# A hybrid attention block on one core: p and its weights prepared among the heads, z by pairs of token tiles, convolution ahead of token sums

## The chip, the core and the metric

The kernel runs on one core of a Trainium2 chip. The metric is the device time of one execution in microseconds (us). The core has a matrix engine (PE), three elementwise engines (DVE, ACT and POOL), an engine that issues transfers (SP), and 16 DMA engines. PE writes its products into banks of 128x512 floats in the accumulation memory (PSUM); a bank can be written again only when whoever reads it is done.

## What is computed

One layer of a streaming encoder on 512 tokens with 1024 features, all in fp32, with x held transposed (features by tokens):

```
h = rms_norm(x);  z = h @ w_in            # q latent | kv latent | rope key | diff q | diff k | diff v
x = x + concat[8 MLA heads, 4 differential heads](z) @ w_out
h2 = rms_norm(x)
x = x + (silu(causal_conv3(h2 @ w_gate)) * (h2 @ w_up)) @ w_down        # 2816 = 22 blocks of 128
x = x + sigmoid(rms_norm(x) @ w_ple_gate) * (p @ w_ple_proj)            # p: 512 x 256
```

The attention is causal by chunks of 64 tokens. For a tile of 128 queries only the keys up to it are computed.

## The kernel before

**Products.** Every large product is made of three (`mm3`, L151): each factor is split into a high part, which PE takes directly, and the rest (low), and PE sums high·high, high·low and low·high (L154 to L156). A split is a cast on ACT (`hi`, `h`) and a subtraction on DVE, or on POOL where `eng=G` stands (`lo`, `l`). `load_w` (L142) loads a raw weight block of 128x1024 and splits it; `hl` (L786) does so in the later stages.

**Order.** PE runs in the order in which the program is written (L98). DVE, ACT and POOL run so only in two regions: from the start to slot 4 of the MLA heads (opened at L218 and closed by `region.__exit__` under `i == 4`), and from the last output products to the end of the token preparation (L792). Outside of them a scheduler orders the three. Each engine works through its own queue in order, so an instruction that waits holds back all behind it.

**Banks and buffers.** PSUM is divided by tags: `acc` 2 banks, `lg` 3, `tp` 2, `ob` 1. SBUF tiles come from pools by tag with a number of buffers each. A load into a buffer waits until the last use of the tile that was there.

**Stages.**
1. Start: `WARM` = 17 small products on ones keep PE busy until the first weights are there. Then `zA` (the latents) over four pairs of feature blocks (`kq`) and four token tiles (`t`).
2. `zd` (the differential heads' q, k, v: three groups `c` of 512 columns) is cut into units of six matmuls by `zd_units` (L398). They fill gaps: `pump(n)` puts n units into PE's order. For c = 1 and 2 the units run token tile by token tile, each over its four weight blocks. `zd_norm(c)` scales group c: a chain of small DVE instructions and four of 128x512.
3. The MLA heads run in 32 slots (head h, query tile t). A slot issues the logits (`ml`) of the next slot, at t = 0 and 1 the transposes of q and k for the next head (`qT`, `kT`, evacuated by ACT and DVE into `st`), then some zd units, the transposes of the probabilities (`pTm`, evacuated as `pt` by ACT or DVE in turn) and the products with v (`mo`). The first three slots also load and split w_d for zd's group 1 (`zw1`), and slot 4 runs `zd_norm(0)`.
4. The differential heads run in 16 slots (`dl`, `pmd`, `pTd`, `do`, transposes `d0T` and `d1T`), with the output projection (`o`, weights `hi_o` and `lo_o`) as filling. The eight last sums of the projection follow, each with `add_x` on DVE and a square on ACT (`nsq`), summed on DVE in `nr`.
5. p and w_ple_proj are split in this last stretch, after the attention's buffers are released; POOL makes their three low parts. `pp_unit(b)` makes the eight products p @ w_ple_proj, which are put aside by ACT (`ppo`) and a store; all of them use the two `acc` banks. Between them lie the norm's products (`norm_r`, `norm_b`), and then DVE and ACT prepare h2 (`tokens`: `xg`, `b1`, `b2`).
6. Feed-forward blocks 0 to 2 (`plain`) take all eight products for g and u. Block 3 and later (`gu_units`) take seven half-sized ones (`11`, `12`, `S2`, `S4`, `S3`, `S1`, `22`), which need sums of tokens (`token_sums`: `bt`) and sums of weights (`w_prep`: `s`, `wT`). `gate_post` is the convolution: it reads the bank of g (ACT `cv`, then two DVE instructions). `up_post` multiplies by u and splits the result (`ah`, `al`). The down projection (`dn`) runs as filling, with weights of `down_w`.
7. The last norm and the gate.

The kv tile (`kvb`: keys and values of the MLA heads) lies in pool `att`; b1, b2 and bt lie in the feed-forward pools.

Of the kernel before, what the change touches and what calls it, by code (L numbers as in the profile page):

```python
# [11 lines left out]
F32 = mybir.dt.float32  # L12
# [43 lines left out]
WARM = 17  # L56
# [38 lines left out]
def hybrid_block(ctx: ExitStack, tc: tile.TileContext, a: dict, out: bass.AP):  # L95
# [6 lines left out]
    sm = ctx.enter_context(tc.tile_pool(name="sm", bufs=2))  # L102
    att = tc.alloc_tile_pool(name="att", bufs=1, side="left")
# [22 lines left out]
    def kv_tile(name, dtype=F32):  # L126
        return att.tile([P, NT, H, 160], dtype, tag="kv", name=name)
# [219 lines left out]
    for kq in range(4):  # L347
        for t in range(NT):
            mm3(zps[t][:, :416], xblocks(2 * kq, 2 * kq + 2, t, *wa[kq], 416), kq == 0, kq == 3)
# [48 lines left out]
    def zd_units():  # L398
        for c in range(3):
# [9 lines left out]
            else:  # L409
                ws = zw1 if c == 1 else [load_w(a["w_d"][c, kq], 1024, f"d{c}{kq}") for kq in range(4)]  # L410
                for t in range(NT):
                    ps = bank("acc", f"zd{c}{t}")
                    for kq in range(4):
                        mm3(ps, xblocks(2 * kq, 2 * kq + 2, t, *ws[kq], 512), kq == 0, kq == 3)
                        if kq == 3:
                            zd_out(c, t, ps)
                        yield
# [296 lines left out]
    for i, (h, t) in enumerate(slots):  # L714
        if i + 1 < len(slots):
            mla_logits(*slots[i + 1])
        if i < 3:
            zw1.append(load_w(a["w_d"][1, i + 1], 1024, f"d1{i + 1}"))
        if i == 4:
            region.__exit__(None, None, None)  # L720
            zd_norm(0)
        if h + 1 < H and t < 2:
            (mla_q, mla_k)[t](h + 1)
# [39 lines left out]
    for dq in (2, 3):  # L763
        wo2[dq] = wo_w(1, dq)
    order = (0, 4, 1, 5, 2, 6, 3, 7)
# [28 lines left out]
    ptw = hl(raw_w(a["pT"], "rA", "pT", bufs=2), "wA", "pT", bufs=2, eng=G)  # L794
    wpp = [hl(raw_w(a["w_pp"][i], "rS", f"pp{i}", bufs=3), ("wS", "wT")[i], f"pp{i}", eng=G) for i in range(2)]
# [15 lines left out]
    for b in order:  # L811
# [7 lines left out]
        square(b)  # L819
    square(None)  # L820
# [26 lines left out]
    def pp_unit(b):  # L847
        ps, w = bank("acc", f"pp{b}"), wpp[b // 4]
# [22 lines left out]
    def w_prep(f):  # L871
# [3 lines left out]
        s24 = ffn2.tile([P, 1024], F32, tag="s24", name=f"s24_{f}")  # L875
        V.tensor_tensor(s24[:, :512], ra[:, :512], rs_[:, 512:], op=ALU.add)
        V.tensor_tensor(s24[:, 512:], ra[:, 512:], s24[:, :512], op=ALU.add)
        w = {"22": hl(raw_w(gu(f, 2, 3), "r22", f, 512), "w22", f, 512)}
        for keys, t in ((("11", "12"), wa_), (("S2", "S4"), hl(s24, "wT", f)), (("S3", "S1"), hl(rs_, "wS", f))):
# [144 lines left out]
    for k in range(K2):  # L1024
        token_sums(k)
# [205 lines left out]
```

## Time and profile before

| | us |
|---|---|
| three timed runs | 678.59, 679.49, 679.68 (median 679.49) |
| the profiled execution | 677.74 |
| its span in the trace | 676.0 |
| mean granted PE clock | 0.986 |

The trace belongs to the profiled execution. Its span begins with the first recorded instruction and ends with the last; 1.74 us of the execution's time lie around it. Times in rows count from the start of the span. A row of a timeline gives the start, the length, the engine, the line, the instruction with what it writes and reads, its shape, and in brackets how long the engine stood idle ahead of it and which instruction released it. A 512-column matmul is recorded with 0.39 us but the next one starts 0.23 us later, since they are pipelined. The clock is the share of full speed that PE was granted.

In order of time, the stages lie at: zA from 7 us, the MLA heads from about 60, the differential heads from about 160, the last sums of the output from 248, the products of p from 256, the feed-forward from 274 and the last gate from about 640.

### The profile page before, as it was taken

The page shows a single profiled execution, that of the slowest core. Times are in us where ns is not written, and L with a number is a line of the kernel's source. Part 1 is how long each engine was busy: PE and PEld are TensorE (multiplying, and loading weights), DVE is VectorE, ACT ScalarE, POOL GpSimd, SP SyncE. Part 2 cuts the span into 40 slices and gives each one's busy share as a digit, 9 for nine tenths or more (in the row PEclk, how much of TensorE's full clock was granted, in tenths as well). Part 3 has the DMA queues.
Part 4 walks back from the last instruction along what each step waited for, and adds up shares of the span by engine and source line. Part 5 has one row for each costly group of instructions (what it writes and reads, how often), then busy time and mean ns, then how long its engine had stood idle before and what let it go on. Part 6 is the DMA issues. An engine that isn't in the chain of part 4 may idle for free.

```text
span 676.0 us, 10426 instructions
## 1 busy us (share of the span) xinstructions
PE 651.0 (96%) x3942; PEld 574.8 (85%) x3942; DVE 495.0 (73%) x938; ACT 359.5 (53%) x623; POOL 64.7 (10%) x94
## 2 busy tenths in 40 slices
PE   9999699999999998989999999999999999999997
PEld 9987488888878786868899999999999999988886
DVE  6989636747779857997867768676868687768543
ACT  7496435636666545755545546464645455546311
POOL 2900040001010031011000010000000000000000
PEclk9999889999999998989999999999999999999999
DMA  8240124305200047656746465655557463431121
GB/s 306 78 157 31 64 80 150 99 1 201 80 1 1 1 157 202 208 134 178 166 119 194 110 172 140 168 150 152 168 119 196 114 196 112 142 125 36 51 85 48
DMA packets 29914, 82.64 MB, mean 122 GB/s; under 512 B 3101, under 2 KB 4125, under 8 KB 29737
## 3 DMA queue, kind: packets, MB, share of 16 engines
q1 hardware_dynamic: 23816, 69.17, 31.3%
q0 software_dynamic: 5616, 12.33, 10.4%
q8 instruction: 31, 0.51, 0.3%
q10 hardware_dynamic: 432, 0.49, 0.2%
q14 instruction: 19, 0.15, 0.1%
HBM read 77.77 MB, written 5.52 MB: 123 GB/s over the span
## 4 chain that ended last, share of the span: by engine, by line
PE 77%; DVE 13%; ACT 6%; issue 2%; DMA 1%; ACTq 0%; DVEq 0%
PE dn L156 6%; PE dn L155 6%; PE dn L154 6%; PE gx L156 4%; PE gx L155 4%; PE gx L154 4%; PE g L154 3%; PE g L155 3%; PE g L156 3%; PE mo L568 2%; PE zd L155 2%; PE pg L154 2%; PE pg L155 2%; PE pg L156 2%; PE zd L156 2%
## 5 line engine op out<-in xcount | busy, mean ns | idle before, releaser
L156 PE MATMUL dn<-ah,lo_dn 128*128 128x512 f32 x144 | 56.2, 390 | 0.0
L155 PE MATMUL dn<-al,hi_dn 128*128 128x512 f32 x144 | 56.1, 390 | 0.0
L154 PE MATMUL dn<-ah,hi_dn 128*128 128x512 f32 x144 | 56.0, 389 | 0.0
L869 POOL DMA_DIRECT2D rS<-in_w_gu x19 | 22.9, 1205 | 266.4 <-DVE lo_dn L148 100.2
L154 PE MATMUL zd<-hi_d,xh 128*128 128x512 f32 x96 | 40.8, 425 | 2.8 <-ACT hi_d L147 2.8
L189 DVE TENSOR_TENSOR wTl<-s,wTh 128x1024 fp32r<-128x1024 f32 x19 | 23.3, 1225 | 27.3 <-ACT wTh L188 27.3
L155 PE MATMUL zd<-lo_d,xh 128*128 128x512 f32 x96 | 39.1, 408 | 1.3 <-DVE lo_d L148 1.3
L616 DVE TENSOR_TENSOR x<-x,dn 128x512 f32<-128x512 f32 x44 | 30.0, 681 | 10.7 <-PE dn L156 10.6
L188 ACT CAST wAh<-rA 128x1024 fp32r<-128x1024 f32 x22 | 23.0, 1046 | 22.1 <-PE g L155 21.4
L997 DVE SCALAR_TENSOR_TENSOR cv<-u,cv 128x512 f32<-128x512 f32 x22 | 15.2, 690 | 25.0 <-PE u L156 25.0
L555 DVE TENSOR_REDUCE nm<-ml 128x1 f32<-128x128 f32 (+3 forms) x32 | 15.5, 486 | 23.8 <-PE ml L156 23.6
L156 PEld LDWEIGHTS dn<-ah,lo_dn 128*128 128x128 f32 x144 | 27.0, 188 | 5.6
L154 PEld LDWEIGHTS dn<-ah,hi_dn 128*128 128x128 f32 x144 | 27.1, 188 | 5.0
L189 DVE TENSOR_TENSOR wAl<-rA,wAh 128x1024 fp32r<-128x1024 f32 x22 | 26.9, 1225 | 6.0 <-ACT wAh L188 6.0
L155 PEld LDWEIGHTS dn<-al,hi_dn 128*128 128x128 f32 x144 | 27.0, 188 | 5.0
L989 ACT ACTIVATE cv<-g,cols 128x512 f32<-128x512 f32 x22 | 17.1, 776 | 24.5 <-DVE g L977 24.5
L189 DVE TENSOR_TENSOR wSl<-rS,wSh 128x1024 fp32r<-128x1024 f32 x21 | 25.7, 1225 | 4.4 <-ACT wSh L188 4.4
L558 ACT ACTIVATE pm<-ml,nm,rq 128x128 f32<-128x128 f32 (+3 forms) x32 | 19.7, 617 | 15.8 <-DVE nm L556 15.7
L188 ACT CAST wTh<-s 128x1024 fp32r<-128x1024 f32 x19 | 19.9, 1048 | 15.0 <-PE g L155 15.0
L661 ACT ACTIVATE pmd<-pmd,nmd 128x128 f32<-128x128 f32 (+3 forms) x32 | 17.9, 559 | 18.8 <-DVE nmd L660 16.7
L154 PE MATMUL g<-b2h,wAh 128*128 128x256 f32 (+1 forms) x88 | 26.3, 299 | 0.7 <-ACT g L960 0.7
L154 PE MATMUL o<-yh,hi_o 128*128 128x512 f32 x64 | 26.7, 418 | 0.0
(469 smaller groups left out, 2268.1 us busy)
## 6 DMA issues: line engine op xcount, KB each, us to landing
rA<-in_w_gu SPq DMA_DIRECT2D x22, 512.0 KB, 3.6
rS<-in_w_gu SPq DMA_DIRECT2D x22, 512.0 KB, 3.6
rS<-in_w_gu POOLq DMA_DIRECT2D x19, 512.0 KB, 6.5
raw_dn<-in_w_down SPq DMA_DIRECT2D x18, 512.0 KB, 6.4
raw_d<-in_w_d SPq DMA_DIRECT2D x12, 512.0 KB, 3.5
r<-in_w_gu SPq DMA_DIRECT2D x19, 256.0 KB, 3.9
raw_o<-in_w_out SPq DMA_DIRECT2D x8, 512.0 KB, 4.2
rS_pg<-in_w_pg SPq DMA_DIRECT2D x6, 512.0 KB, 4.3
```

What stands on the lines that cost most here:

```text
L154: TE.matmul(ps, xh, wh, start=first and i == 0, stop=False, skip_group_check=again)
L155: TE.matmul(ps, xh, wl, start=False, stop=False, skip_group_check=again)
L156: TE.matmul(ps, xl, wh, start=False, stop=last and i == n - 1, skip_group_check=again)
L188: S.copy(h_, src)
L189: return (eng or V).tensor_tensor(l_, src, _f32(h_), op=ALU.subtract)
L555: V.reduce_max(nm, ps[:, :n], axis=AX.X, negate=True)
L558: S.activation(pm[:, :n], ps[:, :n], AF.Exp, bias=nm, scale=r, accum_out=mla["ssum", h // 2][:, t, h % 2:h % 2 + 1])
L616: V.tensor_tensor(xb(b), xb(b), ps, op=ALU.add)
L661: S.activation(pm[:, :n], pm[:, :n], AF.Exp, bias=nm, scale=-1.0, accum_out=s0 if m == 0 else s1)
L869: nc.gpsimd.dma_start(sums[f].rearrange("p (i c) -> p i c", i=2), a["w_gu"][f][:, :2048].rearrange("p (i c) -> p i c", i=2)[:, :, :512], a ...
L989: S.activation(cv, g, AF.Identity, bias=cols[:, C_CB + f:C_CB + f + 1], scale=cw[2])
L997: V.scalar_tensor_tensor(cv, u, sign, cv, op0=ALU.mult, op1=ALU.mult)
```

## The change

It has eight parts; all keep what is computed.

- Five warm-up products fewer, and the first pair of feature blocks of zA runs feature block by feature block over all four token tiles.
- A pool `kvp` of its own holds the kv tile. After the heads the same buffer takes the split p and the first half of w_ple_proj (`pk`), then the high part of the token sums, then that of the last norm's result.
- zd's groups 1 and 2 run by pairs of token tiles: weight block by weight block, over two tiles in two banks.
- `zd_norm(0)` moves from slot 4 to slot 8, behind the next head's k; in the first slots the transposes of q and k stand ahead of the weight loads in the program.
- `pk` is loaded and split (ACT and DVE) before the last output products are written, so that the scheduler puts it among the differential heads. The second half of w_ple_proj is split on DVE and ACT behind the seventh output sum. The eight products use seven banks, and two more of them stand ahead of the norm's second half or between other steps.
- In `w_prep` the sums of weights are made in place, in the raw tile.
- In blocks 0 to 2 the token sums stand behind the convolution, two by two. The loads of down weights wait until a block's `al` is done.
- In block 4 the product `S4` stands ahead of the `22` product of block 3.

```diff
-WARM = 17
+WARM = 12
...
+    kvp = tc.alloc_tile_pool(name="kvp", bufs=1, side="left", reuse_waits="tile")
...
     for kq in range(4):
+        if kq == 0:
+            for j in range(2):
+                for t in range(NT):
+                    mm3(zps[t][:, :416], xblocks(0, 2, t, *wa[0], 416)[j:j + 1], j == 0, False)
         for t in range(NT):
-            mm3(zps[t][:, :416], xblocks(2 * kq, 2 * kq + 2, t, *wa[kq], 416), kq == 0, kq == 3)
+            if kq:
+                mm3(zps[t][:, :416], xblocks(2 * kq, 2 * kq + 2, t, *wa[kq], 416), False, kq == 3)
...
-                for t in range(NT):
-                    ps = bank("acc", f"zd{c}{t}")
+                for t0 in range(0, NT, 2):
+                    ps = [bank("acc", f"zd{c}{t0 + u}") for u in range(2)]
                     for kq in range(4):
-                        mm3(ps, xblocks(2 * kq, 2 * kq + 2, t, *ws[kq], 512), kq == 0, kq == 3)
-                        if kq == 3:
-                            zd_out(c, t, ps)
-                        yield
+                        for u in range(2):
+                            mm3(ps[u], xblocks(2 * kq, 2 * kq + 2, t0 + u, *ws[kq], 512), kq == 0, kq == 3)
+                            if kq == 3:
+                                zd_out(c, t0 + u, ps[u])
+                            yield
...
+        if i == 4:
+            region.__exit__(None, None, None)
+        if i == 8:
+            with tc.issue_after(mla["k"].ins):
+                zd_norm(0)
+        if h + 1 < H and t < 2:
+            (mla_q, mla_k)[t](h + 1)
         if i < 3:
             zw1.append(load_w(a["w_d"][1, i + 1], 1024, f"d1{i + 1}"))
-        if i == 4:
-            region.__exit__(None, None, None)
-            zd_norm(0)
-        if h + 1 < H and t < 2:
-            (mla_q, mla_k)[t](h + 1)
...
+    pk = kvp.tile([P, 4, 1024], F32R, tag="kv", name="pk")
+    for i, (src, name) in enumerate(((a["pT"], "pT"), (a["w_pp"][0], "pp0"))):
+        split(pk[:, 2 * i], pk[:, 2 * i + 1], load_raw(src, 1024, name))
+    ptw, wpp = (pk[:, 0], pk[:, 1]), [(pk[:, 2], pk[:, 3])]
...
-    ptw = hl(raw_w(a["pT"], "rA", "pT", bufs=2), "wA", "pT", bufs=2, eng=G)
-    wpp = [hl(raw_w(a["w_pp"][i], "rS", f"pp{i}", bufs=3), ("wS", "wT")[i], f"pp{i}", eng=G) for i in range(2)]
+    rpp = raw_w(a["w_pp"][1], "rS", "pp1", bufs=3)
...
         square(b)
+        if b == 6:
+            wpp.append(hl(rpp, "wT", "pp1"))
...
-        ps, w = bank("acc", f"pp{b}"), wpp[b // 4]
+        ps, w = bank(("acc", "acc", "lg", "lg", "lg", "tp", "tp", "acc")[b], f"pp{b}"), wpp[b // 4]
...
-        s24 = ffn2.tile([P, 1024], F32, tag="s24", name=f"s24_{f}")
-        V.tensor_tensor(s24[:, :512], ra[:, :512], rs_[:, 512:], op=ALU.add)
-        V.tensor_tensor(s24[:, 512:], ra[:, 512:], s24[:, :512], op=ALU.add)
+        V.tensor_tensor(ra[:, :512], ra[:, :512], rs_[:, 512:], op=ALU.add)
+        V.tensor_tensor(ra[:, 512:], ra[:, 512:], ra[:, :512], op=ALU.add)
...
     norm_r()
-    pp_unit(3)
     next(w0)
-    pp_unit(4)
+    for b in range(3, 6):
+        pp_unit(b)
     norm_b()
-    pp_unit(5)
-    next(tk)
-    next(tk)
-    pp_unit(6)
-    next(tk)
-    next(tk)
-    pp_unit(7)
+    for b in range(6, 8):
+        next(tk)
+        next(tk)
+        pp_unit(b)
...
-        split(ah[f], al[f], cv)
+        done[f] = split(ah[f], al[f], cv)
...
-            ws = down_w(f0, nf, dh)
+            with tc.issue_after(done[f0 + 2].ins):
+                ws = down_w(f0, nf, dh)
...
-    for k in range(K2):
-        token_sums(k)
     for f in range(NPLAIN):
-        if f:
-            if f + 1 < NPLAIN:
-                *_, W[f + 1] = w_plain(f + 1)
-            else:
-                W[f + 1] = w_prep(f + 1)
+        if f and f + 1 < NPLAIN:
+            *_, W[f + 1] = w_plain(f + 1)
+        if f + 2 >= NPLAIN:
+            for k in (0, 1):
+                token_sums(2 * (f + 2 - NPLAIN) + k)
         if f + 3 >= NPLAIN:
             w_sums(f + 3)
+        if f + 1 == NPLAIN:
+            W[f + 1] = w_prep(f + 1)
         plain(f, W[f])
...
         if old:
+            if f == NPLAIN + 1:
+                next(g)
             next(old)
...
-        next(g)
+        if f != NPLAIN + 1:
+            next(g)
         next(g)
```

Three places show how the instructions now stand. First, DVE in the first MLA slots: `nm` are the maxima of a tile's logits (`ml`), `st<-qT` and `st<-kT` the low parts of the next head's q and k, `lo_d` the low parts of w_d's blocks, `rs_` and `rd` the chain of `zd_norm(0)`. Before, from the end of that chain to the third maximum:

```order
L172 SCALAR_TENSOR_TENSOR rs_t<-rs_g,rd 128x32
L173 SCALAR_TENSOR_TENSOR rd<-rs_t,rd 128x32
L396 TENSOR_TENSOR zd_797<-zd_797,rd 128x512
L148 TENSOR_TENSOR lo_d_871<-raw_d_868,hi_d_870 128x1024
L192 SCALAR_TENSOR_TENSOR st<-qT_874,qcol,st 96x512
L528 COPY pt<-pTm_888 128x128
L555 TENSOR_REDUCE nm<-ml_892 128x1
```

And now, from the same st<-qT to the copy of the third tile's probabilities:

```order
L193 SCALAR_TENSOR_TENSOR st<-qT_866,qcol,st 96x512
L149 TENSOR_TENSOR lo_d_876<-raw_d_873,hi_d_875 128x1024
L535 COPY pt<-pTm_887 128x128
L562 TENSOR_REDUCE nm<-ml_891 128x1
L563 TENSOR_TENSOR nm<-nm,rq 128x1
L190 TENSOR_TENSOR st<-kT_900,st 96x512
L149 TENSOR_TENSOR lo_d_910<-raw_d_907,hi_d_909 128x1024
L562 TENSOR_REDUCE nm<-ml_932 128x1
L563 TENSOR_TENSOR nm<-nm,rq 128x1
L149 TENSOR_TENSOR lo_d_944<-raw_d_941,hi_d_943 128x1024
L535 COPY pt<-pTm_953 128x384
```

The chain is gone from here, st<-qT stands ahead of lo_d, and the copy of 384 columns stands directly behind the low part of the fourth weight block.

Second, ACT among the differential heads, in slots 5 to 7: `pmd` are exponentials of a tile, `pt<-pTd` the evacuation of its transposed probabilities, `st<-d1T` that of a head's transposes. Before:

```order
L661 ACTIVATE pmd,s_2061<-pmd,nmd 128x256
L661 ACTIVATE pmd,s_2104<-pmd,nmd 128x256
L526 COPY pt<-pTd_2132 128x512
L661 ACTIVATE pmd,s_2061<-pmd,nmd 128x384
L661 ACTIVATE pmd,s_2142<-pmd,nmd 128x384
L188 CAST st<-d1T_2163 128x512
```

And now:

```order
L668 ACTIVATE pmd,s_2059<-pmd,nmd 128x256
L668 ACTIVATE pmd,s_2102<-pmd,nmd 128x256
L189 CAST pk<-raw_pT 128x1024
L533 COPY pt<-pTd_2130 128x512
L189 CAST st<-d1T_2161 128x512
L668 ACTIVATE pmd,s_2059<-pmd,nmd 128x384
```

The cast of p stands ahead of the copy of 512 columns. Its load is the first that takes over a raw buffer from POOL's second `lo_o`.

Third, DVE at the end of block 0 of the feed-forward: `xg<-xg,xg` and `btl` belong to the token sums, `cv<-g` is the convolution, `wAl` and `wSl` are low parts of weights. Before, the convolution follows the last sum:

```order
L189 TENSOR_TENSOR btl<-xg_3040,bth 128x512
L189 TENSOR_TENSOR btl<-xg_3044,bth 128x512
L990 SCALAR_TENSOR_TENSOR cv<-g_3097,cols,cv 128x511
L189 TENSOR_TENSOR wAl_3160<-rA_3157,wAh_3159 128x1024
L991 SCALAR_TENSOR_TENSOR cv<-g_3097,cols,cv 128x510
```

And now it stands behind the first two instructions of the sums:

```order
L921 TENSOR_TENSOR xg_3027<-xg_3027,xg_2992 128x256
L921 TENSOR_TENSOR xg_3031<-xg_3031,xg_2995 128x256
L190 TENSOR_TENSOR wAl_3123<-rA_3120,wAh_3122 128x1024
L1001 SCALAR_TENSOR_TENSOR cv<-g_3060,cols,cv 128x511
L190 TENSOR_TENSOR wSl_3129<-rS_3126,wSh_3128 128x1024
L1002 SCALAR_TENSOR_TENSOR cv<-g_3060,cols,cv 128x510
```

All other sums have moved behind it.

More of the change, by code (lines that the diff above doesn't have):

```diff
@@ L126, in kv_tile @@
     def kv_tile(name, dtype=F32):
-        return att.tile([P, NT, H, 160], dtype, tag="kv", name=name)
+        return kvp.tile([P, NT, H, 160], dtype, tag="kv", name=name)
     def th_tile(name):
@@ L874, in w_prep @@
         wa_ = hl(ra, "wA", f, bufs=2)
-        s24 = ffn2.tile([P, 1024], F32, tag="s24", name=f"s24_{f}")
-        V.tensor_tensor(s24[:, :512], ra[:, :512], rs_[:, 512:], op=ALU.add)
-        V.tensor_tensor(s24[:, 512:], ra[:, 512:], s24[:, :512], op=ALU.add)
+        V.tensor_tensor(ra[:, :512], ra[:, :512], rs_[:, 512:], op=ALU.add)
+        V.tensor_tensor(ra[:, 512:], ra[:, 512:], ra[:, :512], op=ALU.add)
         w = {"22": hl(raw_w(gu(f, 2, 3), "r22", f, 512), "w22", f, 512)}
-        for keys, t in ((("11", "12"), wa_), (("S2", "S4"), hl(s24, "wT", f)), (("S3", "S1"), hl(rs_, "wS", f))):
+        for keys, t in ((("11", "12"), wa_), (("S2", "S4"), hl(ra, "wT", f)), (("S3", "S1"), hl(rs_, "wS", f))):
             for j, k in enumerate(keys):
@@ L882, in w_prep @@
         return w
-    b1, b2 = (tuple(ffn.tile([P, K2, T], F32R, tag=n + j, name=n + j) for j in "hl") for n in ("b1", "b2"))
-    bt = tuple(ffn2.tile([P, K2, 4, H2], F32R, tag="bt" + j, name="bt" + j) for j in "hl")
+    b1, b2 = (tuple(ffn2.tile([P, K2, T], F32R, tag=n + j, name=n + j) for j in "hl") for n in ("b1", "b2"))
+    bt = kvp.tile([P, K2, 4, H2], F32R, tag="kv", name="bth"), ffn2.tile([P, K2, 4, H2], F32R, tag="btl", name="btl")
     xg = {}
@@ L938, in hybrid_block @@
     tb["11"], tb["21"], tb["22"] = tuple(b[:, :, t1] for b in b1), tuple(b[:, :, t1] for b in b2), tuple(b[:, :, t2] for b in b2)
-    ah, al = {}, {}
+    ah, al, done = {}, {}, {}
     def plain(f, w, mid={}):
@@ L1058, in hybrid_block @@
             for n, i in (("b1", 0), ("b2", 2)):
-                h_, l_ = (ffn.tile([P, 2, 1024], F32R, tag=n + j, name=f"pg{n}{j}") for j in "hl")
+                h_, l_ = (ffn2.tile([P, 2, 1024], F32R, tag=n + j, name=f"pg{n}{j}") for j in "hl")
                 for j in range(2):
@@ L1072, in hybrid_block @@
     assert not fill or next(fill[0], None) is None
-    h3h, h3l = (ffn2.tile([P, NK, T], F32R, tag="bt" + j, name=f"h3{j}") for j in "hl")
+    h3h, h3l = kvp.tile([P, NK, T], F32R, tag="kv", name="h3h"), ffn2.tile([P, NK, T], F32R, tag="btl", name="h3l")
     nr_ = [ffn.tile([P, 1024], F32, tag="raw", bufs=2, name=f"nr3{i}") for i in range(2)]
@@ L1154, in hybrid_block @@
     ffn.release()
+    kvp.release()
     dwn.release()
```

## The prediction

> **What bounds the kernel now.** I began with the page's first and fourth parts, which say which engine is full and which engine the last chain runs through.
>
> ```profile
> PE 651.0 (96%) x3942; PEld 574.8 (85%) x3942; DVE 495.0 (73%) x938; ACT 359.5 (53%) x623; POOL 64.7 (10%) x94
> PE 77%; DVE 13%; ACT 6%; issue 2%; DMA 1%; ACTq 0%; DVEq 0%
> ```
>
> PE is busy for 651.0 of 676.0 us, and no matmul is removed except five warm-up ones. So all that can be won is PE's 25 us of waits and the time in which its clock was lowered. The waits of PE (what PE had next, what released it, us in total, times, the longest) and then three windows (start:end and length, busy us of each engine with its instructions, then the granted clock, DMA share and GB/s) show where both lie.
>
> ```profile
> PE kT L542 <- DVE st L192: 3.3, 1, 3.3
> PE pp L154 <- ACT ppo L852: 3.3, 1, 3.3
> PE zd L154 <- ACT hi_d L147: 2.8, 1, 2.8
> PE g L154 <- DVE cv L991: 2.2, 1, 2.2
> PE u L154 <- DVE u L978: 1.6, 1, 1.6
> PE zd L155 <- DVE lo_d L148: 1.3, 2, 0.7
> ```
>
> ```profile
> 299.00:301.00 2.00, 2.00 (x7) 1.59 (x6) 2.00 (x3) 0.81 (x2) 0.00 (x0) 0.56 0.77 258
> 305.00:330.00 25.00, 22.70 (x165) 21.34 (x164) 19.05 (x24) 12.90 (x21) 1.52 (x2) 1.00 0.72 180
> 350.00:600.00 250.00, 250.00 (x1727) 234.11 (x1726) 188.73 (x245) 134.40 (x198) 15.64 (x13) 1.00 0.55 151
> ```
>
> From 350 to 600 us PE never stops, so the change can only cost there. The waits sit in the MLA slots (kT, zd), at the sums of squares (pp) and where the feed-forward begins (g, u). The clock fell to about half behind g's wait of 2.2 us, which ended at 298 (0.56 from 299 to 301), but not behind u's of 1.6 (1.00 from 305 to 330, where it lies).
>
> **A, the start.** These are rows of the timeline (start, us, engine, line, instruction), as are those in the parts below.
>
> ```profile
> 1.04 6.26 PE L202 MATMUL warm<-ones 128*128 128x128 f32 x34 [1.04 <-DVE ones L198]
> 22.98 0.16 DVE L179 TENSOR_SCALAR rs_m<-ssx 128x4 f32<-128x4 f32 x1 [0.23 <-PE ssx L354]
> ```
>
> Seventeen warm products take 6.26 us (34 records), so five fewer are 1.8 us, of which the first zA products can use about 1.3. But the next thing all depend on, the scale of x, starts on DVE at 22.98 after only 0.23 us of idle: DVE's own queue sets it, and its work is the same. I take 0.2, with bounds 0 and 1.3.
>
> **B, the MLA slots.** What stood ahead of the wanted evacuations was DVE's and ACT's own queue.
>
> ```profile
> 72.31 1.22 DVE L148 TENSOR_TENSOR lo_d<-raw_d,hi_d 128x1024 fp32r<-128x1024 f32 x1
> 73.44 0.74 DVE L192 SCALAR_TENSOR_TENSOR st<-qT,qcol,st 96x512 fp32r<-96x512 f32 x1
> 82.07 0.78 ACT L558 ACTIVATE pm<-ml,nm,rq 128x512 f32<-128x512 f32 x1 [1.46 <-DVE nm L556]
> 82.84 1.98 ACT L147 CAST hi_d<-raw_d 128x1024 fp32r<-128x1024 f32 x2
> 79.13 0.39 PE L154 MATMUL zd<-hi_d,xh 128*128 128x512 f32 x1
> 79.36 0.40 PE L155 MATMUL zd<-lo_d,xh 128*128 128x512 f32 x1
> 86.21 0.63 PE L154 MATMUL zd<-hi_d,xh 128*128 128x512 f32 x1
> 86.64 0.63 PE L155 MATMUL zd<-lo_d,xh 128*128 128x512 f32 x1
> ```
>
> The kT transposes (3.3) need the bank that st<-qT frees at 74.2. Ahead of it stood the zd_norm(0) chain and lo_d. After, ACT's half goes ahead of its weight cast and DVE's ahead of both: about 72.0, so 1.3 of wait is left and 1.9 goes. By pairs, the third and fourth weight blocks are wanted two units later, so hi_d (2.8) and lo_d (1.3) go. That is 6.0 of idle. The clock had been low after both waits: at 86 us zd products stand 0.43 apart instead of 0.23 at 79. Over about 16 of them, and the small products between, I count 4.9. One wait is new. The DVE copy of pt for the third tile now stands behind the fourth lo_d, which waits for ACT's cast, queued behind pm of the fourth tile (0.78): placing these rows in the new order, pt is ready some 2.1 after PE asks for it, and a second copy 0.4 late. Behind pt on DVE stand the maxima of the next two tiles; that is included. Net: 6.0 + 4.9 − 2.5 = **8.4**. Upper bound 9.5, if lo_d comes earlier; lower bound 4.5, if that wait also lowers the clock. The bank changes of the pairs cost nothing: at least one slot's logits lie between a pair's last product and the next pair. The moved zd_norm(0) runs on DVE in slots 8 to 10; if PE's logits wait for maxima behind it, up to 1.
>
> **E, p and w_pp among the differential heads.** ACT gets two 1024-wide casts and DVE two subtractions there.
>
> ```profile
> 191.10 2.39 POOL L148 TENSOR_TENSOR lo_o<-raw_o,hi_o 128x1024 fp32r<-128x1024 f32 x1 [21.86 <-ACT hi_o L147]
> 195.27 0.57 ACT L526 COPY pt<-pTd 128x512 f32<-128x512 f32 x1
> 199.32 0.66 PE L642 MATMUL d0T<-ident,zd 128*128 128x128 f32 x4 [0.49 <-ACT pt L526]
> DMA to landing us min/median/max: 3.4/4.2/9.4
> ```
>
> raw_pT takes the buffer that POOL's lo_o leaves at 193.5, and these loads (the last row, of raw_o) land 3.4 us later at the soonest: 197. ACT meets the cast at 195.3, ahead of the pt copy that PE's do products need, so ACT stands still for 1.6 and is 2.6 late with the cast; PE waits about 1.0 at do and 2.1 instead of 0.49 at d0T. I take **−2.5**: worst −5 with a slower landing (the median already adds 0.8), best 0 if the buffer comes free sooner.
>
> **C, the products of p and the norm.** POOL's three subtractions go, and DVE's adds ran beside them.
>
> ```profile
> 250.80 2.20 DVE L809 TENSOR_TENSOR nr<-nr,nsq 128x512 f32<-128x512 f32 x1
> 256.33 0.68 DVE L809 TENSOR_TENSOR nr<-nr,nsq 128x512 f32<-128x512 f32 x1
> 260.76 0.69 DVE L809 TENSOR_TENSOR nr<-nr,nsq 128x512 f32<-128x512 f32 x1 [0.15 <-ACT nsq L807]
> 262.20 0.79 PE L154 MATMUL pp<-wAhpT,wShpp 128*128 128x512 f32 x1 [3.28 <-ACT ppo L852]
> 264.93 1.03 PE L834 MATMUL nr<-ones,nr 128*128 128x1 f32 x8
> 270.52 1.41 DVE L896 SCALAR_TENSOR_TENSOR xg<-x,cols,nr 128x512 f32<-128x512 f32 x2 [0.18 <-ACT nr L842]
> 272.46 0.69 DVE L898 TENSOR_TENSOR b1l<-xg,b1h 128x512 fp32r<-128x512 f32 x1 [0.53 <-ACT b1h L900]
> 273.82 0.39 PE L154 MATMUL g<-b1h,wAh 128*128 128x512 f32 x1
> ```
>
> This add and a second like it took 2.20 instead of 0.68, so the last add (261.45) comes 3.0 earlier, less one new 1.2 subtraction on DVE: 259.7. The third product takes another bank and no longer waits for ACT; three products (six matmuls of 0.228 each) after the last output block at 256.0 end at 260.1, and the norm's products start there instead of at 264.93. From them to xg were 5.6; three products now stand between the norm's two halves instead of two, and PE becomes the later there by about 1.2: xg at 266.9. The first token tile followed xg by 2.6 (272.46 + 0.69 − 270.52), so the first g comes at 269.5, not 273.82: **4.3**. Bounds 3 (a cast late on ACT) and 5.4 (PE alone decides).
>
> **D, convolution ahead of token sums.**
>
> ```profile
> 285.08 0.76 DVE L907 TENSOR_TENSOR xg<-xg,xg 128x256 f32<-128x256 f32 x2
> 297.96 0.47 PE L154 MATMUL g<-b1h,wAh 128*128 128x512 f32 x1 [2.22 <-DVE cv L991]
> ```
>
> All sums, from 285.08 on, stood ahead of the convolution that frees g(2)'s bank. After, it ends near 284.9, while PE wants the bank near 291: 2.2 of idle and about 1.7 of slow clock go, **3.9** (bounds 0 and 4.2). The sums are needed by the first product of block 3, near 302; DVE is done with them and the splits by about 301, so cover is thin. In block 4 a product of 1.4 moves ahead of the u wait (1.6); an ACT copy of about 0.7 then ends last: **0.9** (0 to 1.6).
>
> **The in-place sums.** Now rA is released after wTl, not after the sum.
>
> ```profile
> 409.48 1.23 DVE L189 TENSOR_TENSOR wTl<-s,wTh 128x1024 fp32r<-128x1024 f32 x1 [1.69 <-ACT wTh L188]
> 412.18 0.33 SPq L783 DMA_DIRECT2D rA<-in_w_gu  x1
> 415.41 0.78 ACT L989 ACTIVATE cv<-g,cols 128x512 f32<-128x512 f32 x1 [1.37 <-DVE g L977]
> DMA to landing us min/median/max: 3.4/3.6/5.2
> ```
>
> A load issued at 410.7 for the block after next lands at 414.3 (3.6, the last row, of rA). ACT meets its cast near 414.0, ahead of the cv at 415.41, whose result waits over 2 us for PE's u. So I cost it at 0 while a load lands within about 6 us.
>
> **Sum.** 0.2 + 8.4 − 2.5 + 4.3 + 3.9 + 0.9 = 15.2. The two new waits of about 2.1 stand between 1.6, which left the clock alone, and 2.2, which didn't: I take 1.0 for one of them. Gain **14.2**, against the profiled execution 677.74 − 14.2 = 663.5 (span 676.0 to about 661.8). That execution was 1.75 under the median of the three runs, so the forecast is **665.3**.
>
> The Trainium skill, "TensorE: Matmul & The Clock Gate", section "Why this matters for your kernels", says that only PE gaps beyond about 3 us throw the clock back. The trace disagrees: after 2.2 us of idle it granted 0.56. By the page's rule the 1.0 would not be subtracted, and the time would be 664.3.
>
> **Rivals.**
> 1. Both new waits lower the clock (B 5.5 instead of 8.4) and raw_pT lands late (E −4): 665.3 + 2.9 + 1.5 − 1.0 = 668.7. For: landings up to 9.4, and an idle of 2.2 was enough. Against: only one of the waits is surely over 2.
> 2. DVE, full from 270 to 309, stays the bound in the plain blocks, and PE waits at block 3 as long as before at block 2: D is 0, 669.2. For: 1 us of cover. Against: two 1.2 us down weights leave that stretch.
> 3. Better: the buffer for raw_pT is early, the pt copy isn't late, the start gives 1: 665.3 − 2.5 − 2.1 − 0.8 − 1.0 = 658.9. For: the scheduler's order leaves lo_d free to run as soon as its cast is done. Against: the rows put that cast behind pm.
> 4. Slower: in the blocks, rA's load comes after the cast's place, ACT stands on it, and cv, then u and the next block wait. Each us beyond 6 from issue to landing costs 1 us in each of 19 blocks; from 0.8 a block (a landing of 6.8) all 14.2 is gone, at 7 us it is 684. Against: the longest rA landing was 5.2; for: the load starts beside POOL's added loads and the down weights.
> 5. The change doesn't do what it says: the new waits fill what the old ones leave, and the time stays within 1.4: 679.
>
> **How the numbers follow.** Forecast 0.44, rival 1 0.20, 2 0.12, 3 0.13, 4 0.07, 5 0.04. The range takes the forecast's bounds with rivals 1 to 3: 658 to 673, leaving out 4, 5 and the tails. Faster by over 0.2% (about what a measurement can tell from no change; 1.4 us) 0.89, same 0.04, slower 0.07.
>
> **What would show it.** Right: kT's wait near 1.3, no wait at hi_d, a wait of 2 at mo for pt; no ppo wait; norm products right behind the third product; g(2) without wait; do and d0T waiting for ACT near 185 to 190. Wrong: waits of zA or u in every block from 350 on (rival 4), or gx of block 3 waiting for DVE (rival 2).

## The result: the forecast gain came, and two waits that nobody had forecast took more

| | median us | runs (lowest to highest) | ratio to before [95% interval] |
|---|---|---|---|
| before | 679.93 | 11 (678.59 to 681.18) | |
| after | 681.96 | 11 (680.77 to 685.50) | 1.0037 [1.002, 1.0053] |
| forecast | 665.3 | | 0.979 |

The change makes the kernel slower by 0.4%, and the forecast was 16.7 us too low. The profiled execution of after is the slowest of its eleven (685.5 us, span 683.7); the one of before (677.74) lies below all eleven of these. So the 7.7 us between the two traces are more than the 2.0 us between the medians. What follows says where they arise.

The first and fourth parts of the page of after, to be held against those of before:

```profile
PE 654.0 (96%) x3932; PEld 577.1 (84%) x3932; DVE 487.9 (71%) x941; ACT 358.2 (52%) x623; POOL 60.5 (9%) x91
PE 70%; DVE 13%; ACT 8%; DMA 4%; issue 4%; POOL 0%; ACTq 0%; DVEq 0%
```

PE has fewer matmuls and is busy for 3 us longer; its mean granted clock is 0.979, where it was 0.986. In the chain, DMA has grown from 1% to 4%. The waits of PE after (what PE had next, what released it, us in total, times, the longest):

```profile
PE pTm L530 <- ACT pt L533: 9.1, 2, 8.9
PE pTm L530 <- ACT pm L565: 3.1, 1, 3.1
PE g L155 <- ACT g L971: 1.7, 2, 1.3
PE mo L575 <- DVE pt L535: 1.2, 1, 1.2
PE kT L549 <- DVE st L193: 1.1, 1, 1.1
PE d0T L649 <- DVE st L190: 1.1, 1, 1.1
```

All the waits that the prediction wanted gone are gone (pp for ppo, g for cv, u, zd) or no longer than it said (kT 1.1 against 1.3, mo for pt 1.2 against 2.1). At the head of the list stand two that it did not have; the third, for ACT's copy of g in blocks 3 and 4, is longest in block 4, where the wait for u went. Windows of after (start:end and length, busy us of each engine, granted clock, DMA share, GB/s) show what follows each of them, and the stretch that the prediction feared:

```profile
121.00:129.00 8.00, 7.20 (x24) 6.29 (x25) 5.57 (x15) 5.25 (x11) 0.00 (x0) 0.50 0.37 117
173.68:183.92 10.24, 10.18 (x43) 9.69 (x44) 3.42 (x8) 3.79 (x11) 0.00 (x0) 0.50 0.18 52
350.00:600.00 250.00, 250.00 (x1743) 234.82 (x1742) 178.59 (x239) 131.04 (x196) 15.89 (x14) 1.00 0.56 152
```

Behind each wait PE runs at half its clock. From 350 us on nothing has changed.

To place the time, the starts of the same matmul in the two traces are subtracted (after minus before, us; below nothing is ahead). The difference between two marks is what the stretch between them lost. The same is done for four of the experiments below: 5 (slots alone), 1 (strip on POOL), 2 and 12. A run of g is a row of neighbouring products into g's bank.

| mark | after | slots alone | strip on POOL | and first lo_o on DVE | both lo_o on DVE |
|---|---|---|---|---|---|
| first logits of the MLA heads | 1.05 | −0.93 | −0.61 | 0.35 | −0.59 |
| first logits of the 4th head | −8.34 | −10.28 | −9.96 | −9.02 | −9.95 |
| of the 5th head | 4.24 | 2.11 | −9.95 | −9.03 | −9.95 |
| of the 8th head | 3.69 | 1.54 | −10.49 | −9.59 | −10.51 |
| second `yT` (end of the MLA heads) | 10.14 | 8.02 | −4.15 | −9.91 | −10.83 |
| third differential head's logits | 13.42 | 7.99 | −1.02 | −8.38 | −11.18 |
| first product of p | 13.70 | 7.97 | −0.76 | −7.57 | −10.56 |
| first g | 9.33 | 9.64 | −5.12 | −11.98 | −14.96 |
| fifth run of g (first on b2) | 11.10 | 9.64 | −3.00 | −8.12 | −12.87 |
| first `gx` of block 3 | 6.96 | 9.61 | −7.12 | −12.25 | −17.00 |
| second `gy` (block 4) | 7.74 | 9.61 | −6.74 | −12.07 | −16.42 |
| last matmul | 7.74 | 9.61 | −6.73 | −12.06 | −16.41 |

After is 9.4 us better off at the fourth head than at the first logits, and loses 12.6 before the fifth head and 6.4 at the end of the MLA heads.

**The first loss.** Timeline rows of DVE, POOL and PE of after (start, us, engine, line, instruction, idle time ahead of it and its releaser):

```profile
107.48 0.56 DVE L535 COPY pt<-pTm 128x384 f32<-128x384 f32 x1 [0.84 <-PE pTm L530]
112.93 0.80 POOL L598 DMA_DIRECT2D strip<-vec  x1 [8.16 <-PE zd L157]
118.56 0.27 DVE L599 MEMSET strip<- 64x256 f32 x1 [10.52 <-DMA strip<-vec]
118.76 0.22 DVE L562 TENSOR_REDUCE nm<-ml 128x1 f32<-128x128 f32 x1
121.80 0.47 PE L530 MATMUL pTm<-ident,pm 128*128 128x128 f32 x1 [8.89 <-ACT pt L533]
```

and the same instructions before:

```profile
106.89 0.80 POOL L591 DMA_DIRECT2D strip<-vec  x1 [7.30 <-PE qT L535]
116.46 0.27 DVE L592 MEMSET strip<- 64x256 f32 x1
```

`strip` is the bias of the differential heads, not wanted before their logits (from 177 us on in the trace of before). A transfer that POOL issues brings it, and DVE then writes a constant into one corner of it. In DVE's order this MEMSET is the 212th row in both kernels, so no difference of the orders pointed there. But DVE now comes to it at 108.04 instead of 116.46 (8.42 earlier), and the transfer is issued 6.04 later. The transfer takes 5.5 us (the view of DMA issues); so it landed at 112.4 before, 4.1 ahead of DVE; now it lands 10.4 behind it (4.1 − 8.4 − 6.0). For 10.5 us DVE stands, and with it the maxima, the exponentials and PE.

Most of the 6.04 comes from the 27 small POOL instructions ahead of it (`vb`), which begin 2.6 later and take 2.6 longer. Their timeline row before:

```profile
89.88 6.41 POOL L586 TENSOR_SCALAR vb<-tab 4x207 f32<-4x207 f32 x27 [54.60 <-DVE ssd L390]
```

and after:

```profile
92.44 9.02 POOL L593 TENSOR_SCALAR vb<-tab 4x207 f32<-4x207 f32 x27 [55.47 <-DVE ssd L396]
```

Both delays come from the slots part of the change itself. What releases POOL is `ssd`, the sum of squares of the first token tile of group 1; by pairs that tile is done with the seventh unit instead of the fourth, and ACT's square of it starts at 90.93 instead of 88.45. And five of the POOL instructions now lie beside the products of the moved `zd_norm(0)` on DVE and a `lo_d`; each lasts about until its neighbour is done, and together they are 2.6 longer. The last of these pairs, where most POOL instructions of this size take 0.20:

```profile
98.41 1.23 DVE L149 TENSOR_TENSOR lo_d<-raw_d,hi_d 128x1024 fp32r<-128x1024 f32 x1
98.56 1.15 POOL L593 TENSOR_SCALAR vb<-tab 4x1 f32<-4x1 f32 x1
```

**The second loss.** Rows of after at the end of the MLA heads:

```profile
170.43 2.34 POOL L149 TENSOR_TENSOR lo_o<-raw_o,hi_o 128x1024 fp32r<-128x1024 f32 x1 [56.70 <-ACT hi_o L148]
170.66 2.12 DVE L563 TENSOR_TENSOR nm<-nm,rq 128x1 f32<-128x1 f32 x1
173.02 0.16 DVE L563 TENSOR_TENSOR nm<-nm,rq 128x1 f32<-128x1 f32 x1
173.74 1.12 PE L530 MATMUL pTm<-ident,pm 128*128 128x128 f32 x4 [3.13 <-ACT pm L565]
```

An instruction on 128x1 numbers takes 2.12 us beside POOL's subtraction and 0.16 without it. Before, POOL's subtraction held such an instruction too:

```profile
166.71 0.15 DVE L556 TENSOR_TENSOR nm<-nm,rq 128x1 f32<-128x1 f32 x1
166.89 2.35 POOL L148 TENSOR_TENSOR lo_o<-raw_o,hi_o 128x1024 fp32r<-128x1024 f32 x1 [59.20 <-DVE nm L556]
167.30 1.96 DVE L556 TENSOR_TENSOR nm<-nm,rq 128x1 f32<-128x1 f32 x1
167.82 0.66 PE L523 MATMUL pTm<-ident,pm 128*128 128x128 f32 x4 [0.89 <-ACT pm L558]
```

But that one belongs to the next tile, with time to spare. The maximum that PE wanted first (166.71) had started 0.18 us ahead of POOL; after, POOL starts 0.23 ahead of it. PE's 0.89 is not POOL's doing: experiment 7 has the subtraction on DVE and the same wait. So PE waits 3.13 instead of 0.89, and behind it come 10.2 us at half the clock (the second of the windows above), which cost the other 4.2 of the 6.4.

### The profile page after: what moved, and what is told of

It reads as the page before. It is cut to its first block, busy times and chain, and to the rows that moved or that the text cites. A ratio compares the mean times of both kernels' runs of the same rounds, so it can differ in the third digit from the quotient of the medians.

```text
span 683.7 us, 10360 instructions
## 1 busy us (share of the span) xinstructions
PE 654.0 (96%) x3932; PEld 577.1 (84%) x3932; DVE 487.9 (71%) x941; ACT 358.2 (52%) x623; POOL 60.5 (9%) x91
## 4 chain that ended last, share of the span: by engine, by line
PE 70%; DVE 13%; ACT 8%; DMA 4%; issue 4%; POOL 0%; ACTq 0%; DVEq 0%
PE dn L157 6%; PE dn L156 6%; PE dn L155 6%; PE gx L157 4%; PE gx L156 4%; PE gx L155 4%; PE g L156 3%; PE g L155 3%; PE g L157 3%; PE mo L575 2%; PE pg L155 2%; PE pg L157 2%; PE pg L156 2%; PE zd L155 2%; PE zd L156 2%
## 5 line engine op out<-in xcount | busy, mean ns | idle before, releaser
L189 ACT CAST wSh<-rS 128x1024 fp32r<-128x1024 f32 x21 | 22.1, 1052 | 39.1 <-PE gy L156 39.1
L190 DVE TENSOR_TENSOR wTl<-rA,wTh 128x1024 fp32r<-128x1024 f32 x19 | 23.3, 1226 | 15.1 <-ACT wTh L189 14.5
L1003 ACT ACTIVATE cv<-cv 128x512 f32<-128x512 f32 x22 | 13.9, 631 | 28.8 <-DVE cv L1002 28.8
L189 ACT CAST wTh<-rA 128x1024 fp32r<-128x1024 f32 x19 | 20.0, 1051 | 14.3 <-PE g L156 10.1
L530 PE MATMUL pTm<-ident,pm 128*128 128x128 f32 x80 | 15.2, 290 | 12.3 <-ACT pt L533 9.1
```

Source lines behind the costliest of these rows:

```text
L189: S.copy(h_, src)
L190: return (eng or V).tensor_tensor(l_, src, _f32(h_), op=ALU.subtract)
L530: TE.transpose(ps[:, tsl[j]], pm[:, tsl[j]], ident)
L1003: S.activation(cv, cv, AF.Silu)
```

## The experiments

My theory after reading the two traces: the slots' gain is real, and by itself it makes both new waits; each can be taken away alone. The rivals: a wait is due to something else in the change, or another takes its place as soon as it goes. Ratios are to before, measured on the same chip. "The kernel of 2" is that of experiment 2.

**1. The strip's constant on POOL**, behind the transfer on POOL's own queue, so that DVE doesn't wait.

```diff
-        V.memset(strip[:64, :, 448:], MASK)
+        G.memset(strip[:64, :, 448:], MASK)
```

> The changed kernel, but the constant of the bias strip is written by POOL behind its own transfer, not by DVE. Theory (the strip's transfer, landed at 118.5, held DVE's queue and with it PE for 8.9 us, and the lowered clock behind it took about 3.7 more): the wait of pTm for ACT's pt is gone and the time falls by 12 to 13, from 681.96 to about 669.5. Rival (the shorter slots owe that time anyway: ACT's casts or the pairs of zd are late next, in the same slots): another wait of 6 us or more shows up before 135 us, and the time stays above 676.

670.70 us, 0.9874 [0.9847, 0.9902]. One line on another engine gives about 11 us (1.0037 − 0.9874 of 679), the loss between the fourth and fifth head is nothing (−9.96, −9.95), and the other wait stays as it was. Its list of waits begins:

```profile
PE pTm L530 <- ACT pm L565: 3.1, 1, 3.1
```

**2. And the first of POOL's two lo_o on DVE.**

```diff
-            w = wo_w(kq, dq, G if kq else V)
+            w = wo_w(kq, dq, G if kq and dq else V)
```

> As the run before, and the first of the two output weights' low parts that POOL makes (2.34 us at 170.4) is made by DVE in 1.22. Theory (a DVE instruction of one column beside POOL's subtraction takes 2.1 instead of 0.16, so the exponentials of the fourth tile are late, PE waits 3.1 and its clock falls): the wait at pTm behind ACT's pm shrinks to 1 or less and the time falls by another 4 to 6. Rival (the maximum is late because ACT and DVE are simply full there): the wait stays at 2 to 3 and the 1.22 us on DVE make it longer: no gain, or a loss of 1.

664.11 us, 0.9783 [0.9757, 0.9809]. The wait falls from 3.1 to 1.2, the loss at the end of the MLA heads goes (−9.59, −9.91), and another 6.6 us are won (670.70 − 664.11, on the same chip). With both mends the time is about the one forecast (665.3), but it is not made up as the forecast was: B gives 9.4 for 8.4, and 3.9 are lost between the first and the fifth run of g, for which the forecast had nothing.

**3. Block 4 as before** (after, without the mends).

```diff
-            if f == NPLAIN + 1:
-                next(g)
             next(old)
...
-        if f != NPLAIN + 1:
-            next(g)
+        next(g)
         next(g)
```

> The changed kernel with the order of products in block 4 as it was before. Theory of the prediction (the new order saves 0.9): 0.9 slower. What the trace of the changed kernel suggests (offset to the kernel before grows by 0.7 from block 3 to block 5, so the new order costs as much as it saves or more): a difference within 1 us, below what three rounds can tell; in the trace the wait of u comes back with about 1.6 and the waits of 0.4 at g go.

683.55 us, 1.0076 [1.0054, 1.0098]. PE's wait for u (1.6) is back, and that for g's copy shrinks from 1.3 to 1.0. From block 3 to block 4 this kernel loses 1.58 (3.34 to 4.92) and after 0.78: the reorder saves 0.8, as forecast (0.9), in a stretch that loses otherwise. The ratios are further apart (1.0076 − 1.0037 of 679 are 2.6 us); the trace shows 0.8 of that.

**4. The start as before**: 17 warm-up products and the old first pair.

```diff
-WARM = 12
+WARM = 17
...
-        if kq == 0:
-            for j in range(2):
-                for t in range(NT):
-                    mm3(zps[t][:, :416], xblocks(0, 2, t, *wa[0], 416)[j:j + 1], j == 0, False)
```

> The changed kernel with 17 warm products and the first pair of zA as before. If the shorter start is what made the first scales 0.9 later (the sum of squares at 22.0 instead of 21.1), the time from the first zA to the first logits is 1.0 shorter here and the total about 1 us less. If that 0.9 is only how the first loads fell in one execution, the first logits come at 67 to 68 in both and the total is the same.

680.78 us, 1.0031 [1.0012, 1.0049], like after. With the changed start, the first logits lie between −0.67 and +1.05 in the profiles taken; here, with the old one, at −0.44. The start is worth nothing that can be seen.

**5. The slots alone**: before, with z by pairs, `zd_norm(0)` at slot 8, and q and k ahead of the weight loads; nothing else (the hunks of the change for `zd_units` and the slots).

> The kernel before with one part of the change alone: pairs of token tiles in zd, zd_norm(0) at slot 8, and q and k transposes ahead of the weight loads. Theory (the slots' gain of 9 to 10 is real, and the gain itself brings DVE to the strip's constant before the strip has landed): up to the fifth head's logits it is 9 to 10 ahead, then PE waits 8 to 9 for pt, the clock falls, and the kernel is 2 to 3 slower than before at the sixth head; whether POOL's subtraction then meets a maximum decides the rest: 679.5 + 2 to 6 in total. Rival (the strip is late because of something else in the change, the kv pool for one): no such wait, and the time is 9 to 10 below the kernel before.

687.30 us, 1.0117 [1.0092, 1.0142]. Alone the part is worse than the whole change: 10.28 ahead at the fourth head, 8.02 behind at the end of the MLA heads, and unchanged up to the products of p. (The last 1.7 come there, behind the old wait for ppo; experiment 8 shows how.) Its waits, of PE and then of DVE:

```profile
PE pTm L524 <- ACT pt L527: 8.9, 2, 8.6
...
PE pTm L524 <- ACT pm L559: 3.1, 1, 3.1
```

```profile
DVE strip L593 <- DMA strip<-vec: 10.3, 1, 10.3
```

Both new waits are there, so nothing else in the change is needed for them. The rival is refuted.

**6. The slots with the two mends** on before (the diffs of 1 and 2).

> Before with the slots part (which alone gave 1.0117) and the two mends: the strip's constant on POOL, the first POOL lo_o on DVE. Theory: the slots' 9 us stay, less what the products of p's own wait of 3.3 and the rest keep: no pt wait of 8.9 and no pm wait of 3.1; offset about -9.5 from ml4 to the end, ratio 0.986 to 0.988. Rival (the slots' gain is lost again later in any case, because DVE's or POOL's own amount of work sets the heads' end): offset -9 at ml4 shrinks to between -4 and 0 by d0T, ratio 0.994 to 1.

669.75 us, 0.984 [0.9802, 0.9878]. The offset is −9.25 at the fourth head, −10.09 at the second `yT` and −10.09 at the last matmul. The slots' gain is carried through whole when nothing stands in its way.

**7. The two mends alone** on before, a control.

> Before with the two mends alone, a control: in before the strip's constant waited for nothing and the first lo_o cost PE 0.9 of wait. Theory (the two waits are made by the slots' earlier place in time): nothing to mend, ratio 0.998 to 1.001. Rival (the mends are a gain of their own whatever the slots do): ratio below 0.996, and then part of what the mended kernels won would not speak for the theory.

678.81 us, 0.9983 [0.9956, 1.0011]. In the old order there was nothing to mend. The 17 us that they bring after the change (1.0037 − 0.9783 of 679) are the price of waits which the change made.

**8. The convolution ahead of the token sums, alone** on before (the change's hunks for `plain`, `done` and the loads of down weights).

> Before, with only the token sums behind the convolution in blocks 0 to 2 (and the down weights' loads waiting for al). Theory: this part is right in size and independent of the heads; PE's wait of 2.2 us for the convolution and the slow clock behind it go, 3.9 us: ratio 0.994, offset -4 from the first gx product to the end, nothing ahead of it. Rival (DVE stays the bound in the plain blocks): PE waits at block 3's first product instead, ratio 0.999 to 1.001.

675.62 us, 0.994 [0.9919, 0.996]. From the fifth run of g to the first gx the offset goes from 1.85 to −2.28: 4.1 us, forecast 3.9, and it stays. Ahead of that, between the first product of p and the first g, this profile loses 2.9, and that of the control 1.7. Both wait 3.28 for ppo, as before does, but the clock stays at half for longer behind it. The windows of these stretches, in before, in the control and here:

```profile
261.68:265.09 3.41, 2.89 (x8) 2.31 (x8) 1.23 (x1) 1.48 (x3) 0.00 (x0) 0.50 1.05 189
261.50:268.33 6.83, 6.83 (x21) 5.67 (x22) 2.87 (x13) 1.38 (x3) 0.00 (x0) 0.50 0.94 256
260.43:270.67 10.24, 9.53 (x26) 7.85 (x27) 4.22 (x14) 3.79 (x7) 0.00 (x0) 0.50 0.72 206
```

**9. p's block written earlier**, behind `y_split(3, …)` and ahead of the differential heads (the kernel of 2 with the loop over `pk` moved up).

> As the second run (strip's constant on POOL, first low part on DVE), and p and the first half of w_ple_proj are written ahead of the differential heads in the program, so that their loads take raw buffers that are free early and the splits stand near the heads' start. Theory (what the heads lose, 2.2 from the second to the fourth, is ACT standing at the cast for a late landing): the offset stays flat there, and the time falls by about 2, to a ratio near 0.975. Rival (the two casts and two subtractions themselves, 4.5 us on ACT and DVE, crowd the heads wherever they stand): no gain, or a new wait near the first head, ratio 0.978 or more.

664.01 us, 0.9779 [0.9755, 0.9804]: no gain. Between the second `yT` and the first product of p the loss shrinks (−7.38 to −6.17, where the kernel of 2 goes from −9.91 to −7.57), but 1.7 are lost ahead of that (−9.08 at the 5th head, −7.38 at the second `yT`). There PE has three small waits for pm, 2.0 in all against one of 1.2 in the kernel of 2, and the clock falls to half behind them:

```profile
158.80:162.21 3.41, 3.41 (x17) 3.41 (x18) 0.49 (x2) 1.79 (x4) 0.00 (x0) 0.50 0.04 14
```

**10. The copies `ppo` in a ring of eight** instead of the shared temporary, in the kernel of 2.

```diff
-        o = t5("ppo")
+        o = dwn.tile([P, T], F32, tag="al", bufs=8, name="ppo")
```

> As the second run, and the copies of the products of p go into eight buffers that are otherwise unused until the first block's end, not into three. Theory (the copy of the seventh product waits 2.1 on ACT for a store to land, the cast of the second token tile behind it is late, PE waits 1.3 and its clock falls: 3.9 between the first and the fifth product of block 0): these 3.9 go, ratio 0.972 to 0.974. Rival (the token tiles come at DVE's pace of 1.3 anyway): a gain below 1.

667.68 us, 0.9841 [0.978, 0.9903]: no gain, against a forecast of 0.972 to 0.974.

**11. Both 9 and 10.**

> Both edits of the two runs before together. If the two causes are separate, their gains add: 5 to 6 below the second run, ratio 0.969 to 0.971, about 658. If time won in the heads is only waited for at the tokens, the gain is that of one.

665.73 us, 0.9803 [0.9781, 0.9826]: no gain either. In 10 the loss from the first to the fifth run of g is gone (−9.76, −9.53; in the kernel of 2 −11.98, −8.12), yet the end is no earlier. Part of that has nothing to do with the edit: the profile of 10 stands 2.2 behind that of 2 at the second `yT` already (−7.74, −9.91), since its clock fell behind a wait that left it alone in 2 (last section). The rest has: PE waits longer for g's copy in blocks 3 and 4, 4.2 in all (1.4 in the kernel of 2), 2.8 of them in block 4. There, in ACT's rows of 10, that copy (the last row) stands behind an activation that waits for DVE's convolution; 5 us earlier ACT waited for the load of a weight block:

```profile
314.82 1.05 ACT L189 CAST wAh<-rA 128x1024 fp32r<-128x1024 f32 x1 [2.48 <-DMA rA<-in_w_gu]
320.27 0.63 ACT L1003 ACTIVATE cv<-cv 128x512 f32<-128x512 f32 x1 [2.27 <-DVE cv L1002]
320.81 0.36 ACT L971 COPY g<-gx 128x256 f32<-128x256 f32 x1
```

The same holds for 11 (−15.76 at the first gx, −11.80 at the end). Here too, time won is waited for at the next place whose input did not come earlier; that the load of rA is what sets it I infer from the first row only.

**12. Both of POOL's lo_o on DVE**, with the strip on POOL.

```diff
-            w = wo_w(kq, dq, G if kq else V)
+            w = wo_w(kq, dq, V)
```

> The changed kernel with the strip's constant on POOL and both POOL subtractions of lo_o on DVE (in the best kernel so far only the first is there). Theory: the loss at the differential heads comes from raw_pT waiting for the buffer that POOL's second lo_o leaves late; with the subtraction on DVE the buffer comes free sooner, the loss of 3.2 between the differential heads' transposes falls to about 1, ratio 0.975 to 0.977. Rival (DVE is too full among the heads): the added 1.2 us on DVE delays the maxima and copies, ratio 0.978 to 0.981, no better than with one of them.

661.41 us, 0.9737 [0.9685, 0.9789]: the lowest median of all (its interval overlaps that of 2), 18.0 us under before and about 20 under after (1.0037 − 0.9737 of 679). Between the second `yT` and the first product of p it loses 0.3, where the kernel of 2 lost 2.3. ACT's timeline row for p's cast in the kernel of 2:

```profile
187.04 1.05 ACT L189 CAST pk<-raw_pT 128x1024 fp32r<-128x1024 f32 x1 [1.58 <-DMA raw_pT<-in_pT]
```

and in this one:

```profile
184.27 0.57 ACT L533 COPY pt<-pTd 128x512 f32<-128x512 f32 x1
185.21 1.05 ACT L189 CAST pk<-raw_pT 128x1024 fp32r<-128x1024 f32 x1 [0.38 <-DMA raw_pT<-in_pT]
```

The buffer is free sooner and, by the scheduler's doing, the copy of pt now stands ahead of the cast. The two came together, so this run can't say how much each is worth. Of the 4.3 between the ends of the two profiles (−12.06, −16.41), 2.1 lie in this stretch. 0.9 are there at the first logits, ahead of the edit, and 1.8 arise between the first and the fifth run of g, where the clock of 12 stayed up (last section).

## Why the prediction was wrong, point by point

Each term of the sum against what its own stretch of the trace gave (gain, us):

| term | forecast | after | from |
|---|---|---|---|
| A, the start | 0.2 | −1.1 | first logits; within the scatter |
| B, the slots | 8.4 | 9.4 | to the 4th head |
| (nothing forecast) | 0 | −12.6 | 4th to 5th head |
| (nothing forecast) | 0 | −6.4 | 8th head to the second `yT` |
| E, p among the heads | −2.5 | −3.3 | to the third differential head |
| C, products of p | 4.3 | 4.4 | to the first g |
| (nothing forecast) | 0 | −1.8 | first to fifth run of g |
| D, the convolution | 3.9 | 4.1 | to the first gx |
| block 4 | 0.9 | −0.8 | to the second gy; the edit itself 0.8 |
| in-place sums | 0 | 0.0 | 7.74 from there to the end |

The two stretches left out, from the 5th to the 8th head and from the third differential head to p, give 0.3 together. The 1.0 that the forecast took off for the clock behind new waits lies within E here: through the slots of B, from 60 to 112 us, the clock of after stayed at 1.00.

- **Most terms were right.** B, C, D and E came within about 1 us of their sizes, and B and D, which experiments took alone (6, 8), by the mechanism given. In B, 6.3 of PE's idle went (forecast 6.0), 1.5 came (2.5), and the rest of the 9.4 is the clock behind the old waits, 4.6 (4.9). E's size is partly luck. The prediction said that ACT stands 1.6 for raw_pT, and that PE waits about 1.0 at do and 2.1 instead of 0.49 at d0T. These are ACT's and PE's rows of after:

```profile
207.38 1.05 ACT L189 CAST pk<-raw_pT 128x1024 fp32r<-128x1024 f32 x1 [1.83 <-DMA raw_pT<-in_pT]
208.96 0.33 PE L530 MATMUL pTd<-ident,pmd 128*128 128x128 f32 x1 [0.89 <-ACT pt L533]
211.30 1.12 PE L649 MATMUL d0T<-ident,zd 128*128 128x128 f32 x4 [1.11 <-DVE st L190]
```

  ACT's wait is as forecast. PE's first wait stands at pTd, ahead of do, and its second is 1.1 and ends with DVE, not with ACT's pt. Both together are 1.5 more than before, where the forecast had 2.6. The rest of the 3.3 is the clock, at half for the 3.4 us from 211.2. In the kernels of 3 and 4 nearly the same waits left the clock at 1.00, and this stretch lost 1.6 and 1.7.

- **The step that failed is B's place in the sum, "0.2 + 8.4 − 2.5 + 4.3 + 3.9 + 0.9 = 15.2".** B's net, "6.0 + 4.9 − 2.5 = 8.4", came. But the new order was followed only through the slots that the edit touches, up to the maxima of the next two tiles, and the 8.4 was then added as if all that comes later moved ahead by as much. What B sets off behind these slots was put at nothing, and cost 12.6 and 6.4. POOL's chain to the strip did not move ahead; it came 6 us later, most of that because of the pairs and the moved `zd_norm(0)`, of which the prediction weighed only what they do to PE. And POOL's subtraction changed places with a maximum. The profile of before had signs of both: the MEMSET at 116.46 behind a transfer issued at 106.89, so 4 us of slack against a gain of 8.4, and a 128x1 instruction of 1.96 us beside POOL's subtraction, while the maximum wanted first had started only 0.18 us ahead of it. Experiment 5 shows that B alone makes both waits, 1 and 2 take them away one at a time, 6 leaves B's gain whole, and 7 shows that the mends win nothing where B isn't.
- **Rivals.** That the whole gain is lost and the time comes out slower had a chance of 0.07, by one mechanism: rA in the blocks. It is refuted, from block 4 to the end the offset moves by no more than 0.01. So is DVE as the bound in the plain blocks, since D came. The fifth, "the new waits fill what the old ones leave", is nearest to what happened, but its waits were not named and it had 0.04.
- **The range** of 658 to 673 was made of the bounds of the terms. No bound in it stood for a wait at a place that the edit does not touch.
- **The clock.** The 1.0 set against the two waits foreseen was for idle times near 2. The two that came were 8.89 and 3.13, and the stretches at half the clock behind them, 7.5 and 10.2 us, cost 3.7 and 4.2 more.

## What to carry to other kernels

When an edit makes a stretch shorter by some microseconds, look downstream of it for every instruction on the queues that gained which waits for something that did not: a transfer, another engine's queue, a buffer. Read the slack of each from the trace of before, and count the gain only up to the smallest slack. Look also for what the edit makes later on the other queues: the moved `zd_norm(0)` on DVE delayed a chain on POOL here. An order that shows no difference at a row doesn't mean that the row is harmless; here a MEMSET that takes 0.27 us and is wanted some 60 us later cost 12.6 on DVE's queue and nothing on that of POOL, which brings its data and was free.

## What the runs showed of the hardware

- A subtraction of 128x1024 on POOL (2.34 us) held a DVE instruction on 128x1 numbers with two inputs in SBUF for 2.12 us; the same instruction takes 0.16. I had used this for the large additions (2.20 for 0.68), not for the smallest instruction, where it costs no less. The Trainium skill, "SBUF — State Buffer", section "Who interferes with whom", says that a DVE instruction with two SBUF inputs contends with a GpSimd (POOL) instruction that reads SBUF. The trace agrees, in both directions: the POOL instruction that takes 0.20 took 1.15 beside DVE's `lo_d`.
- The clock also fell behind a shorter idle time than I knew from before. In the kernel of 2, PE waited 1.32 and, one matmul later, 0.22 for the third run of g (a timeline row of PE, and then the windows from there on):

```profile
266.20 0.50 PE L155 MATMUL g<-b1h,wAh 128*128 128x512 f32 x1 [1.32 <-ACT b1h L914]
...
266.93 0.50 PE L156 MATMUL g<-b1l,wAh 128*128 128x512 f32 x1 [0.22 <-DVE b1l L912]
```

```profile
266.00:268.00 2.00, 1.58 (x5) 1.08 (x6) 1.82 (x3) 1.53 (x4) 0.00 (x0) 0.91 0.94 296
268.00:271.00 3.00, 3.00 (x8) 2.35 (x8) 3.00 (x6) 1.93 (x4) 0.00 (x0) 0.50 0.29 112
```

  Before, a single wait of 1.6 left the clock at 1.00, and in the kernel of 12 the waits at this place, there 1.13 and 0.23, left it so, as its window of that stretch shows:

```profile
255.00:275.00 20.00, 18.64 (x78) 14.30 (x77) 16.37 (x24) 12.55 (x18) 0.00 (x0) 1.00 0.79 243
```

- The length of a wait does not settle what the clock does. At the end of the MLA heads PE waits for pm 1.16 in the kernel of 2 and 1.15 in that of 10. The first left the clock alone, the second halved it for 6.8 us (the row and the window of 2, then those of 10):

```profile
158.49 0.66 PE L530 MATMUL pTm<-ident,pm 128*128 128x128 f32 x4 [1.16 <-ACT pm L565]
158.70:165.53 6.83, 6.66 (x55) 6.24 (x53) 4.77 (x13) 5.13 (x13) 0.00 (x0) 1.00 0.26 84
157.43 0.66 PE L530 MATMUL pTm<-ident,pm 128*128 128x128 f32 x4 [1.15 <-ACT pm L565]
158.70:165.53 6.83, 6.83 (x31) 6.54 (x30) 3.03 (x7) 3.28 (x10) 0.00 (x0) 0.50 0.23 72
```

  In 1 and 4 the waits at pTd and d0T are 0.81 and 1.11, and 0.82 and 1.11: the first pair halved the clock, the second did not. In the clock records of all fourteen traces, every stretch at half the clock between start and end of the execution is 3.4, 6.8, 10.2 or 13.7 us long, which are one to four times 3.41. In before they begin at 73.94, 84.19, 261.68 and 299.22, which are 3, 52 and 11 times 3.41 apart. So it may be that the place of a wait on such a grid decides, beside its length; no run was made to test that. For two single profiles it means that a difference of 2 to 4 us need not come from the edit, as in 8 and 10.
